# A hybrid flow trunk on one core: tile order of small products, row blocks of modulation weights, resident tables and the place of gate loads

## The chip, the cores and the metric

The kernel runs on one core of a Trainium2 chip. The metric is the device time of one execution in microseconds (us), the median of three runs. The core has five engines with an instruction queue each: PE (matrix products, with weight loads shown as PEld), DVE (vector), ACT (scalar and activation), POOL (general vector work) and SP, which here only issues transfers. The program sets the order of each queue. Sixteen DMA engines move data between memory (HBM) and the on-chip memory (SBUF). PE's results go to PSUM, in banks.

## What is computed

One step of a two-layer trunk over 128 context tokens and 1024 latent tokens, 1024 wide. Each layer: RMSNorm, shift and scale from the conditioning (`mod`), one combined input projection, three parallel branches, each with its own SiLU gate, and an output projection with RMSNorm, gate and residual.

```python
mod = silu(cond) @ w_mod + b_mod                    # shift, scale, gate
h = rmsnorm(x, g_pre) * (1 + scale) + shift
z = h @ w_in
o_a = windowed_attention(rope(q), rope(k), v, sink) * silu(ag)   # A
o_b = u * (w_s @ layernorm(v) + b_s) * silu(bg)                  # B
# C, gated DeltaNet in chunks of 64 tokens, forward and backward:
t_mat = inverse(eye + strict_lower(beta * k @ k.T * decay))
u, w = t_mat @ (v * beta), t_mat @ (k * beta * exp(gc))
for each chunk:                                                  # the scan
    v_new = u - w @ state
    o = q_dec @ state + a_qk @ v_new
    state = state * exp(g_last) + k_dec.T @ v_new
x = x + gate * rmsnorm(concat(o_a, o_b, o_c) @ w_out, g_post)
```

Outputs are the context and latent tokens, the context keys and values of each layer and the final states.

## The kernel before

Tokens are nine tiles of 128 (`NT`, eight latent and one context tile, `CTX`). Large products use a pair of 16-bit parts for each factor, so three matmuls per block of the contraction; `load_w` brings weights through one of two staging buffers (`st`, 4 KB per partition, L155) and ACT (L160) and DVE (L161) split them. The small products of branch C are in 32 bits; each of them is two instructions on PE, with two weight loads. `X` holds the normalized input of all tiles and is read by every projection (`proj_tok`, L165, matmuls at L170).

A layer has two strands of work. `chain` is branch C: `c_gates` and `c_features`, then `scan`. In `scan`, each of two head groups needs the inverse of its chunk matrices: `diagonals` (L479) turns 32 x 32 diagonal blocks, `solve` (L503) inverts them in 31 dependent DVE steps, and `inverses` (L516) makes the off-diagonal blocks by two products of 32 x 32 blocks. In these, `sides` (L522) lists four combinations of direction and half; each uses other 32 rows and 32 columns of PE's array, and for each side all L blocks j (16 for the latent chunks of a head group, 4 for the context) follow each other (L525 to L528 and L541 to L544). Between the products ACT and POOL write the negated diagonal inverses into W (L537, L539). Then `steps` (L549) runs through the chunks, 18 per head group.

`fill` is everything else that PE can do meanwhile: `b_branch`, `c_gate`, and `attention` with, in layer 0, the modulation of layer 1 (`mod`, L210) threaded through it. `b_gate` (L823) is done twice, for 128 columns each: it loads its weights into `wb` and projects the nine tiles. `both` orders them: the heavy work (attention) runs until `light` has an entry, then a `b_gate` comes. `lat_solve` (L661) adds the entry in the tenth step of the first head group's solve (`LT`) and in the third step of the second's. `merge` (L1124) interleaves chain and fill by the costs that they yield. From the program so written a scheduler with a time model makes the order in which each engine gets its instructions, so an edit in one place can shift work elsewhere.

`mod` loads w_mod as 256 rows by 512 columns (k2 = 0 to 3), two row blocks per load; row block k uses column tile k % 4 of the array (L245 to L249). In the prologue, for the first two parts of layer 0, 16 loads have buffers of their own (`wm`); the 32 others go through `st`.

The rotary table is loaded per token tile, 64 KB at a time, into `rt`: nine times for the keys (L1018) and 18 times for the queries (L909) of each layer, from SP's queue. The transposes of the attention's probabilities (`PT<-P`, L953) are issued there too. CK, 640 columns of triangle masks and a block of ones, is loaded once in the prologue (`masks`, L123) and stays; its last reader in a layer is L405. `out_layer` (L1044) multiplies by w_out, reading the branches' results back from memory into `OTm` (L1054), two buffers. The pools on the "right" side form a stack; `c0` lies at its bottom and holds the first head group's q and k (`cqk[0]`).

## Time and profile before

| | us |
|---|---|
| median of three runs | 1471.59 |
| lowest, highest | 1468.35, 1475.64 |
| the profiled execution | 1462.98 |
| its span in the trace | 1460.2 |
| PE, DVE, ACT, POOL busy | 1307.0, 941.5, 616.9, 613.4 |

The profile is one execution. Its page gives busy times, forty slices of the span, the queues, the chain of work that ended last, and the costliest groups. Longer answers come from the trace: groups by source line, waits, stretches. A name like `ps<-sv,NA` says which tile an instruction writes and which it reads. Layer 0 is at about 75 to 774 us, layer 1 from there to the end; the last part of each layer is `out_layer`. Small products of the inverses stand at about 295, 360, 535 (layer 0) and 994, 1050, 1224 us (layer 1).

### The profile page before, as it was taken

Reading aid. Unit: us, or ns where it says so; the run is one execution under the profiler, and the core shown is the slowest. Engines: PE = TensorE matmul, PEld = TensorE weight load, DVE = VectorE, ACT = ScalarE, POOL = GpSimd, SP = SyncE. Lnnn points to the kernel's source line nnn. Section 1 sums busy time; section 2 is a strip of 40 time slices with the busy share of each in tenths; the row PEclk is TensorE's granted clock in tenths of the full one; section 3 lists DMA queues with packets and bytes.
Section 4 is the critical chain, followed back from the end, with each engine's and each line's share of the span. In section 5 each row is a group of like instructions: output and inputs, shape, how many; then the busy total and the mean of one; then the engine's idle time right before and its main releaser. Section 6 shows DMA issues by size and latency. Waiting matters only on the chain.

```text
span 1460.2 us, 38255 instructions
## 1 busy us (share of the span) xinstructions
PE 1307.0 (90%) x15479; PEld 1009.7 (69%) x15479; DVE 941.5 (64%) x2230; ACT 616.9 (42%) x1411; POOL 613.4 (42%) x818
## 2 busy tenths in 40 slices
PE   6899989899998699959897999999898769987997
PEld 2665567666667587748786655678787658865886
DVE  2865689987646666753446587687875485767333
ACT  2733454434646116732333444332566313665211
POOL 0761245435556135742132432631668403666200
PEclk8999999999999898969998999999999988998999
DMA  9331044839865117673332122242276311877552
GB/s 358 120 80 55 24 113 106 180 105 222 162 171 87 39 32 144 120 221 76 120 131 84 32 63 68 73 95 64 55 142 120 60 49 40 157 115 166 130 181 103
DMA packets 301562, 162.92 MB, mean 112 GB/s; under 512 B 212622, under 2 KB 277938, under 8 KB 301386
## 3 DMA queue, kind: packets, MB, share of 16 engines
q1 hardware_dynamic: 264301, 127.94, 37.4%
q10 hardware_dynamic: 37085, 32.55, 7.6%
q8 instruction: 121, 1.98, 0.6%
q14 instruction: 55, 0.45, 0.1%
HBM read 95.78 MB, written 24.28 MB: 82 GB/s over the span
## 4 chain that ended last, share of the span: by engine, by line
PE 54%; DVE 14%; DMA 13%; issue 7%; POOL 6%; ACT 4%; SPq 1%; ACTq 0%; DVEq 0%; POOLq 0%
PE ps L170 16%; PE ps L1072 12%; PE ps L312 6%; DMA PT<-P 4%; DMA st<-in_w_in_dram 2%; DMA st<-in_w_mod_dram 2%; PE ps L967 2%; POOL P L951 2%; PE ps L249 2%; DVE y L319 1%; DVE sv L512 1%; PE ps L543 1%; PE ps L527 1%; DVE sv L510 1%; DVE wg L161 1%
## 5 line engine op out<-in xcount | busy, mean ns | idle before, releaser
L170 PEld LDWEIGHTS <-X 128*128 128x128 f16 x3888 | 349.6, 100 | 101.2 <-issue 39.3
L170 PE MATMUL ps<-wg,X 128*128 128x256 f16 x2592 | 328.6, 280 | 10.5 <-DVE wg L161 3.9
L951 POOL TENSOR_TENSOR P<-sS,P 128x512 f16<-128x512 f32 (+2 forms) x144 | 150.9, 1053 | 100.9 <-ACT sS L949 100.2
L1072 PEld LDWEIGHTS <-OTm 128*128 128x128 f16 x1728 | 169.1, 99 | 30.5 <-DMA OTm<-mix_d 8.8
L1072 PE MATMUL ps<-wo,OTm 128*128 128x256 f16 x1296 | 152.1, 276 | 7.6 <-DMA OTm<-mix_d 7.6
L312 PE MATMUL ps<-X,wg 128*128 128x512 f16 (+1 forms) x864 | 146.1, 329 | 1.8 <-ACT wg L160 1.4
L946 DVE CUSTOM_DVE_ANT_0 sS<-ps,am,nsk 128x512 f32<-128x512 f32 (+2 forms) x144 | 95.1, 669 | 49.1 <-POOL P L951 24.6
L948 ACT ACTIVATE P<-sS,nmx 128x512 f16<-128x512 f32 (+2 forms) x144 | 94.0, 660 | 73.0 <-DVE nmx L946 67.4
L312 PEld LDWEIGHTS <-wg 128*128 128x128 f16 x864 | 74.0, 99 | 69.1 <-ACT wg L160 1.8
L170 PE MATMUL ps<-wb,X 128*128 128x256 f16 x864 | 102.5, 279 | 14.4 <-ACT wb L160 12.5
L949 ACT ACTIVATE sS<-sS,nmx 128x512 f32<-128x512 f32 (+2 forms) x144 | 95.1, 660 | 4.2 <-DVE OTA L1001 0.4
L145 POOL TENSOR_TENSOR rs<-ms,mhalf 128x1 f32<-128x1 f32 x36 | 20.7, 576 | 171.9 <-DVE ms L1081 103.7
L967 PE MATMUL ps<-Vt,PT 128*128 128x128 f16 (+1 forms) x992 | 67.9, 211 | 22.8 <-DMA PT<-P 21.8
L319 DVE SCALAR_TENSOR_TENSOR y<-zT,cw,y 128x1156 f32<-128x1156 f32 x48 | 68.9, 1439 | 27.4 <-ACT y L317 26.8
L512 DVE TENSOR_TENSOR sv<-sv 128x31 f32<-128x31 f32 (+15 forms) x186 | 78.4, 421 | 4.1
L967 PEld LDWEIGHTS <-PT 128*128 128x128 f16 x992 | 51.1, 100 | 41.6 <-DMA PT<-P 29.7
L510 DVE TENSOR_TENSOR sv<-sv 128x31 f32<-128x31 f32 (+15 forms) x186 | 74.8, 402 | 4.0
L942 PE MATMUL ps<-KT,qT 128*128 128x128 f16 (+2 forms) x272 | 68.6, 269 | 0.0
L288 DVE TENSOR_SCALAR hf<-ps,AB 128x128 f32<-128x128 f32 x117 | 39.7, 402 | 39.3 <-PE ps L281 39.0
L1075 ACT ACTIVATE sq<-ps 128x512 f32<-128x512 f32 x36 | 21.3, 594 | 99.8 <-PE ps L1072 56.8
L941 PE MATMUL ps<-KT,qT 128*128 128x128 f16 (+2 forms) x272 | 60.3, 271 | 3.6 <-DVE nmx L946 1.8
L161 DVE SCALAR_TENSOR_TENSOR wg<-st,wg 128x1024 f16<-128x1024 f32 x44 | 56.0, 1280 | 10.6 <-ACT wg L160 10.4
(265 smaller groups left out, 2723.8 us busy)
## 6 DMA issues: line engine op xcount, KB each, us to landing
st<-in_w_in_dram ACTq DMA_DIRECT2D x38, 512.0 KB
st<-in_w_mod_dram SPq DMA_DIRECT2D x32, 512.0 KB
OTm<-mix_d SPq DMA_DIRECT2D x18, 512.0 KB
wm<-in_w_mod_dram SPq DMA_DIRECT2D x16, 512.0 KB
xt<-in_x_sample_dram SPq DMA_DIRECT2D x16, 512.0 KB
st<-in_w_out_dram ACTq DMA_DIRECT2D x16, 512.0 KB
mix_d<-OTA SPq DMA_DIRECT2D x36, 128.0 KB
xs<-xt SPq DMA_DIRECT2D x9, 512.0 KB
```

The source lines that it names most:

```text
L161: V.scalar_tensor_tensor(dst[:, 4 * h:4 * h + 4, 1, :cols], s, WS, hi, op0=ALU.mult, op1=ALU.subtract)
L170: T.matmul(ps, X[:, t, k, a, :], wg[:, k, b, c0:c0 + n], start=(i == 0), stop=(i == 23))
L312: T.matmul(ps[:, 0:n], wg[:, k, b, 128 * hg:128 * hg + 128], X[:, t0:t1, k, a, :], start=(i == 0), stop=(i == 23))
L319: V.scalar_tensor_tensor(y, zT[:, tap:tap + 1156], cw[:, tap * 6 + ct:tap * 6 + ct + 1], y, op0=ALU.mult, op1=ALU.add)
L510: V.tensor_tensor(t3, m3[:, 0:m, m:m + 1].to_broadcast([128, m, w]), y3[:, m:m + 1, m:32].to_broadcast([128, m, w]), op=ALU.mult)
L512: V.tensor_tensor(y3[:, 0:m, m:32], y3[:, 0:m, m:32], t3, op=ALU.subtract)
L946: V.tensor_tensor_reduce(sS[:, 0:nk], ps[:, 0:nk], mk, -0.125, nsk[:, hh:hh + 1], ALU.add, ALU.min, accum_out=nmx[:, h:h + 1])
L948: S_.activation(P16[:, 0:nk], sS[:, 0:nk], AF.Exp, bias=nmx[:, h:h + 1], scale=-1.0)
L949: S_.activation(sS[:, 0:nk], sS[:, 0:nk], AF.Exp, bias=nmx[:, h:h + 1], scale=-1.0, accum_out=sm[:, h:h + 1])
L951: G.tensor_tensor(P16[:, nk:2 * nk], sS[:, 0:nk], P16[:, 0:nk], op=ALU.subtract)
L967: T.matmul(pops[:, 128 * h:128 * h + n], PT[:, a * nb + j, :], Vt[:, blist[j], kv].rearrange("p s d -> p (s d)")[:, 0:n], start=(i == 0), ...
L1072: T.matmul(ps[:, 256 * i:256 * i + 256], OTm[:, k, a, :], w[:, k, b, :], start=(n == 0), stop=(n == 23))
```

## The change

In `inverses` the two loops are exchanged: for each block j the four sides follow each other, so that consecutive matmuls use four different tiles of the array. In `mod`, loads through `st` take 512 rows by 256 columns, four row blocks, and each feeds four matmuls of 256 columns on the four column tiles; the `wm` loads are as before. CK leaves the permanent pool and is loaded by `c_gates` in each layer, ahead of `sab`; the prologue loads only the part that makes `triL16`, beside the other masks. The rotary table of all nine tiles is loaded once per layer when `attention` starts (`rts`, 4608 bytes per partition). `b_gate` yields after its weight load is written down; `both` then lets heavy work of a cost of 8.0 (first gate) or 1.0 (second) go ahead of the rest of it. The second gate's entry in `light` comes before the solve's first step instead of in its third. The output of `b_gate` goes out in one transfer per pair of tiles. `OTm` becomes the halves of one tile `OT2` that takes the place of `cqk[0]`, and `c0` stays open through `out_layer`.

```diff
@@ -40,6 +40,7 @@
 PRO = 1
 LT = 9
 AHEAD = 6
+EARLY = (8.0, 1.0)
 FILL = 0.9
 
 
@@ -110,10 +111,6 @@
     V.tensor_copy(id16, ident)
     idb = per.tile([128, 128], BF16, name="idb")
     V.tensor_copy(idb, ident)
-    CK = per.tile([128, 640], F32, name="CK")
-    triI = [CK[:, 0:128], CK[:, 128:256]]
-    triL = [CK[:, 256:384], CK[:, 384:512]]
-    bdones = CK[:, 512:640]
     selc = per.tile([128, 2], F32, name="selc")
     V.reduce_sum(selc, ident.rearrange("p (j c) -> p c j", c=32)[:, 0:2, :], axis=AX.X)
     triIc16 = per.tile([128, 2, 64], F16, name="triIc16")
@@ -121,12 +118,12 @@
     triL16 = per.tile([128, 2, 128], F16, name="triL16")
 
     def masks():
-        dma(CK, cst[:, 0:640])
-        ctmp = stg.tile([128, 256], F32, tag="st", name="ctmp")
-        dma(ctmp, cst[:, 640:896])
+        ctmp = stg.tile([128, 512], F32, tag="st", name="ctmp")
+        dma(ctmp[:, 0:256], cst[:, 640:896])
+        dma(ctmp[:, 256:512], cst[:, 256:512])
         G.tensor_copy(triIc16, ctmp[:, 0:128].rearrange("p (r c) -> p r c", r=2))
         G.tensor_copy(mneg, ctmp[:, 128:256].rearrange("p (r c) -> p r c", r=2))
-        G.tensor_copy(triL16, CK[:, 256:512].rearrange("p (r c) -> p r c", r=2))
+        G.tensor_copy(triL16, ctmp[:, 256:512].rearrange("p (r c) -> p r c", r=2))
 
     mhalf = per.tile([128, 18], F32, name="mhalf")
     G.memset(mhalf, -0.5)
@@ -239,14 +236,20 @@
                 for k2 in range(4):
                     if wmp is not None and part < 2:
                         st = wmp.tile([128, 4, 256], F32, tag="wm", name=nm("wm"), bufs=16)
-                    else:
-                        st = stg.tile([128, 4, 256], F32, tag="st", name=nm("st"))
-                    s = st.rearrange("p a b -> p (a b)").rearrange("p (k c) -> p k c", k=2)
-                    dma(s, w_mod[l, 256 * k2:256 * k2 + 256, 512 * cb:512 * cb + 512].rearrange("(k p) c -> p k c", p=128))
-                    for kk in range(2):
-                        k = 2 * k2 + kk
-                        j = k % 4
-                        T.matmul(ps[32 * j:32 * j + 32, :], csp[:, k, :], s[:, kk, :], start=(k < 4), stop=(k >= 4))
+                        s = st.rearrange("p a b -> p (a b)").rearrange("p (k c) -> p k c", k=2)
+                        dma(s, w_mod[l, 256 * k2:256 * k2 + 256, 512 * cb:512 * cb + 512].rearrange("(k p) c -> p k c", p=128))
+                        for kk in range(2):
+                            k = 2 * k2 + kk
+                            j = k % 4
+                            T.matmul(ps[32 * j:32 * j + 32, :], csp[:, k, :], s[:, kk, :], start=(k < 4), stop=(k >= 4))
+                        continue
+                    ch, kq = k2 // 2, k2 % 2
+                    c0 = 512 * cb + 256 * ch
+                    st = stg.tile([128, 4, 256], F32, tag="st", name=nm("st"))
+                    dma(st, w_mod[l, 512 * kq:512 * kq + 512, c0:c0 + 256].rearrange("(k p) c -> p k c", p=128))
+                    for j in range(4):
+                        T.matmul(ps[32 * j:32 * j + 32, 256 * ch:256 * ch + 256], csp[:, 4 * kq + j, :], st[:, j, :],
+                                 start=(kq == 0), stop=(kq == 1))
                 mp = mp_.tile([128, 512], F32, tag="mp", name=nm("mp"), bufs=2 if PIPE else 1)
                 (V.tensor_copy if wmp is not None and part < 2 else S_.copy)(mp, ps)
                 todo.append((part, cb, mp))
@@ -354,6 +357,11 @@
 
     def c_gates(l, cp, gp, out):
         GB = cp.tile([128, 2, 2, 9, 4], F32, name=nm("GB"))
+        CK = gp.tile([128, 640], F32, name="CK")
+        dma(CK, cst[:, 0:640])
+        triI = [CK[:, 0:128], CK[:, 128:256]]
+        triL = [CK[:, 256:384], CK[:, 384:512]]
+        bdones = CK[:, 512:640]
         wab = gp.tile([128, 8, 2, 16], F16, name="wab")
         sab = gp.tile([128, 8, 16], F32, name="sab")
         dma(sab, w_in[l, :, C_AB:C_AB + 16].rearrange("(k p) c -> p k c", p=128))
@@ -522,8 +530,8 @@
             sides = [(r, half, 64 * half + (0 if half == r else 32), 64 * half + (32 if half == r else 0))
                      for r in range(2) for half in range(2)]
             ps = psw()
-            for (r, half, p1, p2) in sides:
-                for j in range(L):
+            for j in range(L):
+                for (r, half, p1, p2) in sides:
                     T.matmul(ps[p2:p2 + 32, 32 * j:32 * j + 32], W[p1:p1 + 32, r, j, p2 % 64:p2 % 64 + 32],
                              PQ[1 if half == r else 0][p1:p1 + 32, L * r + j, :], start=True, stop=True)
             C_ = ep[:, 3328:3840]
@@ -538,8 +546,8 @@
                     else:
                         G.tensor_scalar(dst, src, -1.0, None, op0=ALU.mult)
             ps = psw()
-            for (r, half, p1, p2) in sides:
-                for j in range(L):
+            for j in range(L):
+                for (r, half, p1, p2) in sides:
                     T.matmul(ps[p1:p1 + 32, 32 * j:32 * j + 32], C_[p2:p2 + 32, 32 * j:32 * j + 32],
                              W[p2:p2 + 32, r, j, p2 % 64:p2 % 64 + 32], start=True, stop=True)
             for (r, half, p1, p2) in sides:
@@ -660,9 +668,11 @@
 
         def lat_solve(hg, sv):
             M, Y = diagonals(sv, Ws[hg], 16)
+            if hg:
+                light.append(hg)
             yield 4.0
             for i, cost in enumerate(solve(sv, M, Y)):
-                if i == (2 if hg else LT):
+                if not hg and i == LT:
                     light.append(hg)
                 yield cost * share[5 if hg else 2]
             inverses(sv, Ws[hg], 16, Y)
@@ -825,6 +835,7 @@
         cs = slice(128 * k, 128 * k + 128)
         w = bp.tile([128, 8, 2, 256], F16, name=nm("wb"), bufs=1)
         load_w((w_in[l, :, C_BU + 128 * k:C_BU + 128 * k + 128], w_in[l, :, C_BG + 128 * k:C_BG + 128 * k + 128]), 256, w)
+        yield 0.0
         sc = IWS * IWS * IWS * 0.5
 
         def out(ts, th):
@@ -836,8 +847,7 @@
             src = pt[:, 0:128 * n].rearrange("p (q c) -> p q c", c=128)
             S_.activation(ot[:, 0:n, 0, :], src, AF.Copy, scale=sc)
             V.scalar_tensor_tensor(ot[:, 0:n, 1, :], src, sc, ot[:, 0:n, 0, :], op0=ALU.mult, op1=ALU.subtract)
-            for j, t in enumerate(ts):
-                dma(mix_d[t, :, 4 + k].rearrange("p s c -> p (s c)"), ot[:, j].rearrange("p s c -> p (s c)"))
+            dma(mix_d[ts[0]:ts[0] + n, :, 4 + k].rearrange("t p s c -> p t (s c)"), ot[:, 0:n].rearrange("p t s c -> p t (s c)"))
 
         prev = None
         for ts in pairs:
@@ -883,6 +893,8 @@
             am = p1.tile([128, 640], F32, name="am")
             dma(am, amask)
             sk = p1.tile([128, 8], F32, name="sk")
+            rts = p1.tile([128, 9, 128], F32, name="rts")
+            dma(rts, rope.rearrange("t p c -> p t c"))
             ordert = [CTX] + list(range(8))
             dma(sk, attn_sink[l].partition_broadcast(128))
             nsk = p1.tile([128, 8], F32, name="nsk")
@@ -905,8 +917,7 @@
                 pq = psp()
                 proj_tok(pq[:, 0:256], t, wq)
                 proj_tok(pq[:, 256:512], t, wa)
-                rt = p2.tile([128, 128], F32, tag="rt", name=nm("rt"))
-                dma(rt, rope[t])
+                rt = rts[:, t, :]
                 qa = rope_tile(p2, pq[:, 0:256], 4, rt)
                 th = p2.tile([128, 256], F32, tag="ga", name=nm("ga"), bufs=5)
                 S_.activation(th, pq[:, 256:512], AF.Tanh, scale=IWS * 0.5)
@@ -1014,8 +1025,7 @@
                         for t in ordert:
                             ps = psp()
                             proj_tok(ps[:, 0:256], t, wkv)
-                            rt = p2.tile([128, 128], F32, tag="rt", name=nm("rt"))
-                            dma(rt, rope[t])
+                            rt = rts[:, t, :]
                             ka = rope_tile(p2, ps[:, 0:128], 2, rt)
                             vf = p2.tile([128, 256], F32, tag="ga", name=nm("vf"), bufs=5)[:, 0:128]
                             S_.activation(vf, ps[:, 128:256], AF.Copy, scale=IWS)
@@ -1041,16 +1051,17 @@
                         weigh(*pend.pop(0))
                     finish(p2, *prev.pop())
 
-    def out_layer(l, wo, nextAB):
+    def out_layer(l, wo, c0, nextAB):
         last = l == NL - 1
         with pool(f"o1{l}", 1, "right") as p1, pool(f"o2{l}", 2, "right") as p2:
             wo.append(load_w(w_out[l, :, 512:768], 256, p1.tile([128, 8, 2, 256], F16, name=nm("wo"))))
             wo.append(load_w(w_out[l, :, 768:1024], 256))
             GG, todo = {}, []
+            OT2 = c0.tile([128, 2, 8, 2, 128], F16, tag="cq0", name=nm("OT2"))
 
             for ti, t in enumerate((3, 4, 2, 5, 1, 6, 0, 7, 8)):
                 cond = 1 if t == CTX else 0
-                OTm = p1.tile([128, 8, 2, 128], F16, tag="OTm", name=nm("OTm"), bufs=2)
+                OTm = OT2[:, ti % 2]
                 dma(OTm, mix_d[t])
                 if cond not in GG:
                     g = p1.tile([128, DM], F32, tag="GG", name=nm("GG"), bufs=2)
@@ -1156,7 +1167,7 @@
         rs = ExitStack()
         ctx.enter_context(rs)
         c0 = rs.enter_context(pool(f"c0{l}", 1, "right"))
-        cqk = [q.tile([128, 9, 2, 128], F32, name=nm("cqk")) for q in (c0, cp)]
+        cqk = [q.tile([128, 9, 2, 128], F32, tag=f"cq{i}", name=nm("cqk")) for i, q in enumerate((c0, cp))]
         cv_ = [q.tile([128, 9, 128], F32, name=nm("cv")) for q in (c0, cp)]
         nxt = [None, None]
         light = []
@@ -1194,7 +1205,16 @@
                     yield got
                 elif k < 2:
                     with pool(f"bg{l}{k}", 2, "right") as bp:
-                        yield from b_gate(l, bp, k)
+                        gate = b_gate(l, bp, k)
+                        yield next(gate)
+                        n = 0.0
+                        while n < EARLY[k]:
+                            got = next(heavy, None)
+                            if got is None:
+                                break
+                            n += got
+                            yield got
+                        yield from gate
                     k += 1
                 else:
                     break
@@ -1204,8 +1224,8 @@
             for _ in pairs:
                 next(fl)
         merge(chain(), fl)
+        out_layer(l, wo, c0, nxt[1])
         rs.close()
-        out_layer(l, wo, nxt[1])
         keep.close()
         ls.close()
         vt, AB = nxt
```

## Rows read from the trace of the kernel before

**Rows 1.** The page: busy times and instructions; busy tenths in forty slices.
```profile
PE 1307.0 (90%) x15479; PEld 1009.7 (69%) x15479; DVE 941.5 (64%) x2230; ACT 616.9 (42%) x1411; POOL 613.4 (42%) x818
...
PE   6899989899998699959897999999898769987997
```

**Rows 2.** Stretches: length, busy PE, PEld, DVE, ACT, POOL; clock, DMA share, GB/s.
```profile
236.00:360.00 124.00, 114.14 (x1093) 77.99 (x1091) 113.89 (x289) 52.42 (x132) 52.47 (x64) 0.99 0.68 159
360.00:377.00 17.00, 17.00 (x348) 13.85 (x346) 6.24 (x16) 7.95 (x20) 7.59 (x8) 1.00 0.67 133
494.00:535.00 41.00, 31.67 (x293) 27.66 (x294) 36.99 (x88) 7.77 (x16) 5.61 (x6) 0.83 0.18 53
535.00:555.00 20.00, 20.00 (x317) 16.40 (x314) 7.55 (x15) 8.13 (x16) 9.57 (x16) 0.74 0.21 53
613.00:653.00 40.00, 23.84 (x398) 19.35 (x398) 22.94 (x57) 16.39 (x36) 20.28 (x32) 0.73 0.73 198
1049.00:1068.00 19.00, 18.51 (x336) 16.50 (x337) 9.15 (x24) 9.92 (x22) 9.30 (x9) 0.82 0.32 50
1171.00:1187.00 16.00, 4.81 (x83) 4.04 (x84) 12.04 (x29) 4.80 (x7) 0.76 (x2) 0.70 0.08 22
1224.00:1244.00 20.00, 20.00 (x326) 16.80 (x323) 7.68 (x22) 8.01 (x22) 5.97 (x14) 0.74 0.30 72
```

**Rows 3.** Groups by line: xcount | busy us, mean ns | idle before, releasers.
```profile
L543 PE MATMUL ps<-NA,sv 32*32 32x32 f32 x512 | 18.0, 200 | 0.0
...
L527 PE MATMUL ps<-sv,NA 32*32 32x32 f32 x512 | 17.4, 199 | 1.3 <-DVE sv L520 1.3
...
L527 PE MATMUL ps<-sv,NAc 32*32 32x32 f32 x64 | 1.8, 194 | 0.0
...
L249 PEld LDWEIGHTS ps<-st,csp 128*32 128x32 f32 x128 | 4.3, 109 | 14.3 <-DMA st<-in_w_mod_dram 10.8 <-issue 2.6
```

**Rows 4.** Timeline, weight loads and POOL: start us, us, engine, line, operation.
```profile
308.09 0.16 PEld L249 LDWEIGHTS ps<-st,csp 128*32 128x32 f32 x8 [0.21 <-issue]
...
357.24 4.60 POOL L539 TENSOR_SCALAR NA<-sv 32x512 f32<-32x512 f32 x3
...
360.17 3.82 PEld L527 LDWEIGHTS ps<-sv,NA 32*32 32x32 f32 x128 [0.21 <-issue]
...
379.52 0.31 PEld L566 LDWEIGHTS ps<-ident,qk 64*64 64x64 f32 x8 [0.21 <-issue]
```

**Rows 5.** Timeline of PE: two groups of modulation matmuls.
```profile
308.09 1.07 PE L249 MATMUL ps<-st,csp 128*32 128x512 f32 x8
...
370.01 1.05 PE L249 MATMUL ps<-st,csp 128*32 128x512 f32 x4
```

**Rows 6.** The chain that ended last, two weight loads: start us, us, what.
```profile
190.44 4.86 DMA st<-in_w_in_dram
...
316.86 3.86 DMA st<-in_w_mod_dram
```

**Rows 7.** Waits of SP (us, times, longest), then two pieces of the chain.
```profile
SPq L909 <- DVE ru L870: 25.5, 10, 5.5
...
943.84 3.65 DMA sk<-in_attn_sink_dram
...
1149.65 2.54 DMA rt<-in_rope_dram
```

**Rows 8.** Waits of PE, the chain, PE's timeline at the second gate.
```profile
PE ps L170 <- ACT wb L160: 12.5, 3, 5.7
...
1182.68 1.98 DMA out_dram<-S
...
1186.03 0.80 PE L170 MATMUL ps<-wb,X 128*128 128x256 f16 x3 [5.74 <-ACT wb L160]
```

**Rows 9.** The chain at the start of out_layer and of layer 1.
```profile
650.02 3.55 DMA OTm<-mix_d
...
771.15 2.28 DMA sab<-in_w_in_dram
```

## The prediction

> **What bounds the kernel now.** I read the page first: PE is busy for 1307.0 of 1460.2 us, DVE for 941.5, and the forty slices show PE at 9 nearly everywhere, with dips [rows 1]. So a microsecond of PE work taken away should be worth most of a microsecond, except where something else is late. The table of stretches shows where [rows 2]. From 236 to 360 us DVE is busy 113.9 of 124 us beside PE's 114.1: the 31-step solve and the attention's vector work share the limit. At 360 to 377 and 535 to 555, around the small products of the inverses, PE is busy the whole time, and what waits for them (the scan's steps) can't go on. At 494 to 535 and 1171 to 1187 PE has holes; at 613 to 653 the scan's own chain of latencies ends the layer with PE busy 23.8 of 40 us, so work saved ahead of it is partly lost there. The waits and the chain that ended last name the holes: the gate weights, the modulation loads, a rotary table.
>
> **Small products in another order.** The two products of `inverses` cost 17.4 + 18.0 us for the four 16-block calls and 1.8 us each for the two 4-block calls (one of these two equal rows is shown): 39.0 us of PE for 1152 matmuls, each with its weight load (every source matmul is two instructions) [rows 3]. Today all blocks of one tile of the array follow each other: 128 loads in 3.82 us, 30 ns each [rows 4]. The change lets four tiles with different rows and columns alternate. Nearest rows: eight loads on two alternating 64x64 tiles take 0.31 us with the last one's tail, about 24 ns each without it although each load is twice as wide [rows 4]; eight on four column tiles of the modulation take 0.16 us, and with a last load of 0.109 us off that is 0.05 us for seven, 7 ns [rows 3, 4]. And eight modulation matmuls on four tiles last 1.07 us where four on two tiles last 1.05 [rows 5]: tiles run beside each other. The bounds are 30 ns (no gain) and 7 ns (1152 x 7 = 8.1 us, 31 us saved). No row shows how fast PE's sequencer supplies 128 pairs in a row, so I take 12 ns, nearer to the four-tile row since that is the same case: 13.8 us, 25 us of PE saved. A loss of 1 us is not excluded, since the first four matmuls now need the inputs of all four sides. Not all of it reaches the end. The second product needs POOL's copies at L539, which in one instance end at 357.24 + 4.60 = 361.84, only 1.7 us after the first product began [rows 4], and attention matmuls stand between the two in PE's queue. I count 60%: **15 us** (-1 to 31).
>
> **Clock around them.** The granted clock is 0.74 at 535 to 555 and 1224 to 1244, and 0.82 at 1049 to 1068 [rows 2]; with levels of 1.2 and 2.4 GHz, 0.74 of 20 us means 10.4 us at the low one. In these stretches PE had just run these 32x32 products; at 360 to 377 the same products ran and the clock stayed at 1.00. Shorter products might keep it up: at most half of (10.4 + 10.4 + 6.8) us = 14 us; I take **4** (0 to 14).
>
> The Trainium skill, TensorEngine Tiling (Array Packing), section Restrictions and Gotchas, says that different row tiles cannot use the same PSUM bank at the same time, and all four tiles here write one bank. By that rule the products would stay at 30 ns and the sum would lose these 19 us. The trace speaks against it as far as it goes: the two 64-row tiles of L566 also write one bank, at 24 ns for doubly wide loads [rows 4]. The same skill, TensorE: Matmul & The Clock Gate, section "Wait — 56ns, not 53.3ns?", gives a floor of about 25 ns from start to start of matmuls however small; by it a product would take 128 x 25 = 3.2 us, an estimate from that page, and the saving would be a sixth. The eight loads at 7 ns contradict it for short bursts; no row shows a long one.
>
> **Modulation in four row blocks.** 32 loads change (the `st` ones; the 16 of the prologue's `wm` don't). A load now feeds four instructions on two tiles that hold PE for 1.05 us [rows 5]. Half the columns on four tiles makes it about 0.6 (0.15 to 0.2 of a group is the tail of its last instruction, the rest halves), by the x8 row, in which four tiles cost no more than two. The timeline has 26 such groups and 3 of eight, where two loads came together and nothing is gained: 26 x 0.45 = 11.7 us of PE. Nine groups lie after 360 us, where PE is the limit (4 us); 17 lie in 236 to 360, where DVE limits as well; of their 7.6 us I count a fifth. The load's runs shrink from 2 KB to 1 KB. A 512 KB w_mod load of 2 KB runs took 3.86 us on the chain and a w_in load of 1 KB runs 4.86 [rows 6]; both had other traffic beside them, so I count 0.5 us lost in all. **5 us** (-6 to 11.7; the low end is 32 loads that land 0.2 us later each with PE waiting).
>
> **Rotary tables.** 54 loads (27 per layer) leave SP's queue. One of them stands on the chain with 2.54 us [rows 7], and before such loads SP waited 25.5 us for the buffer's last reader (L870) [rows 7], with transposes of P and qT queued behind; most of that was hidden. I take 3 (0 to 8). Against it: 576 KB per layer now stand ahead of `sk` in SP's queue, and `sk` is already late once, 3.65 us on the chain, with DVE's `nsk` and all DVE work behind it waiting [rows 7]. A load of about that size takes 4 to 5 us by itself; overlapped with `sk` I take 2 (0 to 8 for two layers). Net **+1**. The gate's output goes out in one DMA per pair, 36 issues become 20: off the chain, nothing.
>
> **Early gate weights.** PE waited 12.5 us for the first half of `wb` [rows 8], 5.74 of it before 1186.03 in layer 1 and nearly as much before 504.4 in layer 0. The loads had been issued long before; what held the conversion back was the tile's memory: on the chain the store of the final state, `out_dram<-S`, 1.98 us, ends right before it in layer 1 [rows 8]. That stays. What is new is that one unit of attention (a head or a projection, 1 to 5 us of PE) comes between the load and the gate's matmuls, and fills the hole. For the first gate, 8 units come between, for a wait of some 1 us. So 4 of 5.7 twice, plus 1, two thirds of it at the end: **6 us** (0 to 13). The attention moved ahead carries DVE work beside the solve; at 494 to 535 DVE has 4 us free [rows 2], which covers it; without that cover it costs 2 us per layer.
>
> **Constants.** CK is now loaded in each layer ahead of `sab` in SP's queue. In layer 1 `sab` is on the chain with 2.28 us [rows 9]; 320 KB ahead of it cost at most the 3.86 us of a 512 KB load [rows 6] and at least one issue, about 0.4. The `wab` matmuls wait for X anyway, so I take 1 per layer: **-2** (0 to -8). `triI` and the others are needed much later.
>
> **OT2.** The two halves of one tile replace two buffers. If halves are followed separately, as for X, this costs nothing: what hides a load is the previous tile's matmuls.
>
> **Sum.** 15 + 4 + 5 + 1 + 6 - 2 = 29 us. The profiled execution took 1462.98 us (span 1460.2), so it would take 1434; the median of the three runs is 1471.59, 8.6 above it, and 29 below that is **1443**.
>
> **Rivals.** (1) *The array or its supply does not take four tiles at once.* For: one bank, and no long row. Against: rows 4 and 5. The products stay as they are: 1443 + 19 = 1462. (2) *PE is freed where it only waits.* For: 613 to 653, where the chain and not PE is late, and DVE's 92% at 236 to 360. Then a quarter of the sum stays, 7 us: 1465. Against: PE fully busy around all products. (3) *Everything counts*: products near 7 ns, the clock up, gate holes closed: 31 + 8 + 8 + 3 + 10 - 2 = 58 us at most; with part of it, 1420. (4) *Slower: OT2 is followed as one tile.* Then from the second tile of `out_layer` on, each load waits until the matmuls of the tile before have read the other half. A load takes 3.55 us on the chain [rows 9]; 8 per layer exposed, 16 x 3.55 = 57 us, less the 29: 1500. It decides if the load of one tile is issued after the last matmul of the tile before. Against: slices of X are written in the prologue while matmuls read others, so slices are followed one by one there.
>
> **How the numbers follow.** The kernel's runs tell 0.5% (7 us) from no change. Forecast (1430 to 1457): 0.46. (3): 0.12. (1): 0.14, two thirds of it beyond 0.5%. (2): 0.12, within or just beyond it. (4): 0.08. The remaining 0.08 is for instruction orders of the planner, which I can't price, all slower. Faster 0.46 + 0.12 + 0.09 + 0.02 = 0.69, same 0.15, slower 0.16. The range from 1420 to 1476 leaves out (4), the unpriced cases and a little of (3).
>
> **What would show it.** Each product's 128 loads should take about 1.5 us instead of 3.82, with starts on four tiles; 3.2 or more means rival 1. Clock near 1 at the four stretches. Modulation groups about 0.55 us. PE's wait for `wb` under 4 us in all. No wait on `rt`. `sk` and `sab` no more than 2 us later. OTm loads issued during the tile before. The forecast is wrong if PE's busy time falls by over 25 us and the span doesn't, or if the second product still starts some 6 us after the first.

## The result and the profile after

The changed kernel takes **1431.39 us** (median of four runs, 1427.35 to 1437.79) against 1473.62 for the kernel before (four runs beside it): a ratio of **0.969, 95% interval 0.966 to 0.973**. The forecast was 1443, between 1420 and 1476, and 29 us gained; the medians give 42. The two profiled executions differ by 28.6 us of span (1460.2 and 1431.6), since the profiled execution of before was among the shortest of that kernel's; the comparisons below go by medians and ratios.

The page after: span, busy times, PE's forty slices and the granted clock in tenths.

```profile
span 1431.6 us, 38343 instructions
...
PE 1267.3 (89%) x15607; PEld 979.3 (68%) x15607; DVE 940.3 (66%) x2230; ACT 613.7 (43%) x1411; POOL 604.3 (42%) x818
...
PE   6899979778989789969898999999899768987997
...
PEclk8999999989999989989999999999999989999999
```

PE's busy time fell by 39.7 us [rows 1], more than the span. PE's time that isn't busy (span less busy) went from 153.2 to 164.3 us. The groups of PE by line after: xcount | busy us, mean ns | idle before.

```profile
L251 PE MATMUL ps<-st,csp 128*32 128x256 f32 x256 | 23.6, 414 | 13.5 <-DMA st<-in_w_mod_dram 13.5
...
L551 PE MATMUL ps<-NA,sv 32*32 32x32 f32 x512 | 6.9, 194 | 0.0
L535 PE MATMUL ps<-sv,NA 32*32 32x32 f32 x512 | 6.2, 204 | 4.1 <-DVE sv L528 4.1
...
L535 PE MATMUL ps<-sv,NAc 32*32 32x32 f32 x64 | 0.9, 194 | 0.0
```

L535 and L551 are the old L527 and L543: 39.0 us became 14.9 (the second 4-block row is equal to the one shown). L251 is the old L249 with half the columns: 23.6 us where it was 31.4 in the same view of before:

```profile
L249 PE MATMUL ps<-st,csp 128*32 128x512 f32 x128 | 31.4, 619 | 8.8 <-DMA st<-in_w_mod_dram 8.8
```

The stretches around the large products and the two second gates: length, busy PE, PEld, DVE, ACT, POOL, clock, DMA share, GB/s.

```profile
343.00:373.00 30.00, 26.57 (x482) 17.37 (x480) 17.37 (x42) 18.68 (x43) 16.43 (x15) 0.94 0.84 177
494.00:528.00 34.00, 24.34 (x227) 21.16 (x228) 30.45 (x73) 5.64 (x10) 2.22 (x3) 0.80 0.20 59
530.00:550.00 20.00, 20.00 (x409) 16.85 (x408) 14.52 (x31) 10.82 (x21) 12.82 (x17) 1.00 0.23 59
1020.00:1040.00 20.00, 15.91 (x375) 12.89 (x373) 17.23 (x37) 13.14 (x31) 13.25 (x13) 0.91 0.50 74
1150.00:1165.00 15.00, 5.85 (x45) 4.38 (x46) 13.10 (x31) 2.65 (x4) 0.00 (x0) 0.54 0.22 60
1196.00:1216.00 20.00, 15.04 (x363) 12.24 (x362) 11.57 (x34) 11.68 (x29) 7.36 (x16) 0.91 0.48 107
```

The clock around the second head group's products is 1.00 and 0.91 where it was 0.74 twice [rows 2]. The two holes before the second gate are still there, at 0.80 and 0.54.

Waits of PE after (line, what it waited for: us in all, times, longest), and the chain that ended last just before the second gate of layer 1 (start, us, what):

```profile
PE ps L978 <- DMA PT<-P: 31.7, 33, 2.5
PE ps L251 <- DMA st<-in_w_mod_dram: 13.5, 8, 7.5
PE ps L167 <- ACT wb L157: 11.3, 2, 5.6
...
PE ps L1083 <- DMA OT<-mix_d: 3.6, 3, 1.7
```

```profile
1157.01 1.98 DMA out_dram<-S
1159.15 1.06 ACT wb L157
1160.24 1.24 DVE wb L158
1161.52 3.55 PE ps L167 x17
```

The wait for `wb` went from 12.5 to 11.3 us only [rows 8]: the store of the final state still ends right before ACT's conversion. The wait for w_mod rose from 8.8 to 13.5, the one for the transposed probabilities (`PT`) from 21.8 to 31.7.

**A way to split the time.** Each run has its span and its mean granted clock. Span times clock is the time with the low-clock stretches counted at half; span times (1 - clock) is the rest, called the *loss* here. It is a way of counting, not a law. Over 47 runs of the kernel before, the span falls by some 11 us for each 0.01 of clock (correlation -0.72); if all of the loss were time lost it would fall by some 16 (1473 / 0.943 x 0.01). So the name claims too much: part of the loss falls where PE waits anyway. In the trace of the changed kernel, cut into slices of 10 us, PE's busy time in each times (1 - its clock) makes 44 us, of 67 us of loss. Medians of the runs, in us; the last column is the ratio to the kernel before in the same comparison, and its interval:

| kernel | time | span x clock | loss | ratio |
|---|---|---|---|---|
| before (14, 16 and 17 runs in the three comparisons) | 1473 to 1478 | 1387 to 1388 | 85 to 87 | 1 |
| changed | 1431.4 | 1363.5 | 67 | 0.969 (0.966 to 0.973) |
| side_major | 1473.0 | 1376 | 94 | 0.998 (0.995 to 1.001) |
| old_mod | 1452.1 | 1370 | 80 | 0.984 (0.978 to 0.989) |
| gate_old | 1444.8 | 1372 | 71 | 0.980 (0.976 to 0.984) |
| first_gate_late | 1446.2 | 1373 | 71 | 0.981 (0.977 to 0.984) |
| rt_tiles | 1433.7 | 1370 | 62 | 0.972 (0.968 to 0.976) |
| state_copy | 1436.3 | 1364 | 72 | 0.974 (0.970 to 0.977) |
| out_per_tile | 1432.0 | 1359 | 72 | 0.972 (0.967 to 0.976) |
| two_tiles | 1434.5 | 1366 | 66 | 0.973 (0.968 to 0.978) |
| three_times | 1487.3 | 1390 | 95 | 1.008 (1.005 to 1.010) |
| dense_before | 1458.8 | 1376 | 78 | 0.988 (0.984 to 0.993) |
| before_products | 1455.0 | 1382 | 74 | 0.988 (0.982 to 0.993) |
| before_mod | 1469.4 | 1383 | 86 | 0.997 (0.994 to 0.999) |

Effects below are differences of ratios times 1474 us; against the changed kernel they are known to some 7 to 9 us either way, both intervals put together. Nearly half of the whole gain, 18 to 20 of 42 to 45 us, is loss that went (85 to 87, now 67).

### The profile page after: what moved, and what is told of

It is laid out like the page before. It is cut to its first block, busy times and chain, and to the rows that moved or that the text cites. A ratio compares the mean times of both kernels' runs of the same rounds, so it can differ in the third digit from the quotient of the medians.

```text
span 1431.6 us, 38343 instructions
## 1 busy us (share of the span) xinstructions
PE 1267.3 (89%) x15607; PEld 979.3 (68%) x15607; DVE 940.3 (66%) x2230; ACT 613.7 (43%) x1411; POOL 604.3 (42%) x818
## 4 chain that ended last, share of the span: by engine, by line
PE 46%; DVE 19%; DMA 14%; POOL 8%; issue 8%; ACT 4%; SPq 1%; DVEq 0%; POOLq 0%; ACTq 0%
PE ps L167 12%; PE ps L1083 12%; PE ps L315 7%; DMA PT<-P 6%; POOL P L962 3%; DVE sv L518 3%; DVE sv L520 3%; DMA st<-in_w_in_dram 3%; PE ps L728 2%; PE ps L978 1%; DVE sS L957 1%; DVE y L322 1%; PE ps L601 1%; DVE wg L158 1%; PE ps L590 1%
## 5 line engine op out<-in xcount | busy, mean ns | idle before, releaser
L1083 PEld LDWEIGHTS <-OT 128*128 128x128 f16 x1728 | 169.5, 99 | 26.5 <-DMA OT<-mix_d 4.1
L1083 PE MATMUL ps<-wo,OT 128*128 128x256 f16 x1296 | 153.7, 278 | 3.6 <-DMA OT<-mix_d 3.6
L167 PE MATMUL ps<-wb,X 128*128 128x256 f16 x864 | 101.2, 278 | 12.2 <-ACT wb L157 11.3
L978 PE MATMUL ps<-Vt,PT 128*128 128x128 f16 (+1 forms) x992 | 66.5, 208 | 32.8 <-DMA PT<-P 31.7
L518 DVE TENSOR_TENSOR sv<-sv 128x31 f32<-128x31 f32 (+15 forms) x186 | 74.5, 401 | 4.2
L520 DVE TENSOR_TENSOR sv<-sv 128x31 f32<-128x31 f32 (+15 forms) x186 | 72.7, 391 | 4.5
L157 ACT ACTIVATE wg<-st 128x1024 f16<-128x1024 f32 x44 | 45.3, 1054 | 40.5 <-DMA st<-in_w_in_dram 30.6
L1086 ACT ACTIVATE sq<-ps 128x512 f32<-128x512 f32 x36 | 21.3, 593 | 95.1 <-PE ps L1083 54.7
```

Of the source, the lines that this page charges most:

```text
L167: T.matmul(ps, X[:, t, k, a, :], wg[:, k, b, c0:c0 + n], start=(i == 0), stop=(i == 23))
L518: V.tensor_tensor(t3, m3[:, 0:m, m:m + 1].to_broadcast([128, m, w]), y3[:, m:m + 1, m:32].to_broadcast([128, m, w]), op=ALU.mult)
L520: V.tensor_tensor(y3[:, 0:m, m:32], y3[:, 0:m, m:32], t3, op=ALU.subtract)
L978: T.matmul(pops[:, 128 * h:128 * h + n], PT[:, a * nb + j, :], Vt[:, blist[j], kv].rearrange("p s d -> p (s d)")[:, 0:n], start=(i == 0), ...
L1083: T.matmul(ps[:, 256 * i:256 * i + 256], OTm[:, k, a, :], w[:, k, b, :], start=(n == 0), stop=(n == 23))
```

## The products: undone, and alone

**side_major.** The two loops back in the old nesting, in the changed kernel:

```diff
-            for j in range(L):
-                for (r, half, p1, p2) in sides:
+            for (r, half, p1, p2) in sides:
+                for j in range(L):
```

> The changed kernel with the two loops of the inverses back in the old nesting (all blocks of one side after each other), everything else as changed. Theory T1 (the products' own time is the main gain; 24 us of PE are saved and 60% or more of them reach the end, and the clock around them rises): PE is busy 22 to 26 us longer, a run of 128 loads takes 3.8 us again instead of 1.1, the time is 1431 + 15 to 24 = 1446 to 1455 us, and the low-clock stretches at about 540 and 1230 us come back. Rival R1 (PE was freed where it only waits, and the gain came from the order of work that the other parts bring): PE busy longer by as much, but the time 1431 to 1437.

Measured: 1473.0 us, 42 more than the changed kernel. The whole gain is gone, twice as much as T1 expected. PE is busy 1305.9 us, 38.6 more, of which the products are 26.7 (14.9 in the changed kernel, 41.6 here with two rows of 1.8 for the small calls):

```profile
L551 PE MATMUL ps<-NA,sv 32*32 32x32 f32 x512 | 19.5, 202 | 0.0
L535 PE MATMUL ps<-sv,NA 32*32 32x32 f32 x512 | 18.5, 203 | 4.5 <-DVE sv L528 4.5
```

The other 12 us are the same work taking longer, which fits the lower clock (0.939 for 0.953). Of the 42 us, 13 are span times clock and 27 are loss. The stretches around its four large products, and then one call's weight loads in the timelines of this kernel and of the changed one:

```profile
345.00:375.00 30.00, 30.00 (x402) 21.58 (x399) 13.02 (x27) 12.85 (x28) 12.80 (x11) 0.77 0.52 129
540.00:560.00 20.00, 20.00 (x323) 16.31 (x322) 8.22 (x18) 7.49 (x14) 10.66 (x15) 0.75 0.15 35
1050.00:1070.00 20.00, 18.32 (x299) 15.82 (x300) 8.98 (x19) 9.01 (x20) 9.78 (x9) 0.63 0.12 22
1232.00:1252.00 20.00, 20.00 (x353) 17.34 (x352) 6.51 (x19) 6.96 (x17) 6.08 (x14) 0.91 0.24 49
```

```profile
542.10 3.82 PEld L535 LDWEIGHTS ps<-sv,NA 32*32 32x32 f32 x128 [0.21 <-DVE th L864]
```

```profile
535.91 1.18 PEld L535 LDWEIGHTS ps<-sv,NA 32*32 32x32 f32 x128 [0.21 <-DVE th L864]
```

The first two lie between the same neighbours (`th` at L864 ends the wait before both). In the old order the loads start 29 ns apart, in the new one 8.4 ns (1.07 us from the first to the last of 128). In these four stretches the old order loses 30 x 0.23 + 20 x (0.25 + 0.37 + 0.09) = 21 us to the clock, the changed kernel 30 x 0.06 + 20 x (0 + 0.09 + 0.09) = 5 us: these 16 us are most of the 22 or 23 by which the two profiled executions differ in loss (0.061 x 1472.4 = 90 and 0.047 x 1431.6 = 67).

**before_products.** The same exchange in the kernel before, and nothing else.

```diff
-            for (r, half, p1, p2) in sides:
-                for j in range(L):
+            for j in range(L):
+                for (r, half, p1, p2) in sides:
```

> The kernel before with the loops of the inverses exchanged and nothing else. T1: PE busy falls by 24 us and the time by 15 to 24 us: 1450 to 1459 (ratio 0.984 to 0.990). Rival R1 (the gain needs the other parts): less than 6 us, 1468 or more.

Measured: 1455.0, 18 us faster than before (11 to 26), as T1 said; PE is busy 19.7 us less. R1 falls here and in side_major: the products carry gain in either kernel. But they carry 18 us in one and 42 in the other: the parts don't add up.

## What the slow products did to the clock

The old order holds PE longer and leaves most of the array idle. Which of the two brings the clock down? Two kernels hold PE for longer in the new order.

**three_times.** Each product three times over:

```diff
-            for j in range(L):
+            for j in [j for _ in range(3) for j in range(L)]:
```

> The changed kernel with each of the inverses' products done three times over in the new order (the same blocks into the same places), so that a 16-block call holds PE for about 3 x 1.1 = 3.3 us, nearly as long as the 3.8 us of the old order; everything else as changed. With the old order in the changed kernel the time was 1473, the span times the granted clock 1376 us (changed: 1364) and the rest, lost to the low clock, 94 us (changed: 67). Theory T2 (what the old order costs beside PE's time is the clock: 32x32 products one tile at a time bring it down): span times clock 1373 to 1376, the loss stays at 65 to 72, the time 1440 to 1447. Rival R4 (a longer product brings the loss however its tiles are ordered, by later work and other gaps): the loss rises to 85 to 94 and the time to 1460 or more. Rival R5 (PE's time here is hidden): 1434 or less.

Measured: 1487.3, a loss of 94.5. By the numbers this is R4, but the run didn't make what it was meant to. PE's weight loads of one call, in the timeline:

```profile
1057.18 2.04 PEld L535 LDWEIGHTS ps<-sv,NA 32*32 32x32 f32 x233 [2.44 <-DVE sv L528]
1061.73 1.23 PEld L535 LDWEIGHTS ps<-sv,NA 32*32 32x32 f32 x128 [2.51 <-issue]
1065.74 0.41 PEld L535 LDWEIGHTS ps<-sv,NA 32*32 32x32 f32 x23 [2.79 <-issue]
```

After 233 loads no new one starts for 2.51 us, and after 128 more for 2.79, with nothing in the profile that it waits for; such waits are 12.6 us at L535 and 14.4 at L551. A call took 8 to 11 us instead of 3.3, with holes in it, so it says nothing on a full queue of small products. What PE waits for there no run shows.

**dense_before.** Full-array work instead:

```diff
             ps = psw()
+            for _ in range(3 if L == 16 else 1):
+                w = 448 if L == 16 else 128
+                T.matmul(ps[:, 0:w], ident, C_[:, 0:w], start=True, stop=True)
```

(and the same with `PQ[0]` ahead of the first product).

> The changed kernel with dense work ahead of each of the inverses' products: three full 128x128 by 448-column matmuls in 32 bits (one of 128 columns for the small calls) into the places that the product then overwrites, so that PE is held about as long as the old order held it (some 2.7 us more per large call, an estimate from the modulation's 512-column instructions), but with a full array; the products stay in the new order. Theory T2 (what costs the clock is PE holding on to small products, one tile or stalled, with most of the array idle; as much dense work doesn't): PE busy 20 to 25 us longer, span times clock 1378 to 1390, the loss stays at 60 to 72, the time 1443 to 1458. Rival R4 (any longer hold there raises the loss, by what comes later and by other gaps): the loss at 85 or more, as in the old order (94) and the threefold products (94.5), and the time at 1465 or more.

Measured: 1458.8 us, 28 more than the changed kernel, 14 less than the old order; the intervals don't overlap. The dense work held PE for 21.3 us (the 2.7 us per large call that I had estimated were 2.5). Span times clock is 1376, as in the old order, so PE's time costs 12 to 13 us in both, some 60% of the dense work's and half of the products', give or take the 5 us that another order of work is worth (last section of runs). The loss is 78, between the two theories. The stretches around its products:

```profile
345.00:375.00 30.00, 28.82 (x490) 18.65 (x488) 19.95 (x45) 19.52 (x44) 18.34 (x19) 0.96 0.95 192
535.00:555.00 20.00, 19.84 (x383) 15.34 (x382) 10.74 (x26) 10.16 (x18) 11.91 (x17) 1.00 0.32 87
1030.00:1050.00 20.00, 16.70 (x375) 11.93 (x377) 16.19 (x34) 13.57 (x31) 12.53 (x13) 1.00 0.47 73
1210.00:1230.00 20.00, 18.14 (x365) 13.14 (x363) 8.90 (x31) 10.59 (x29) 8.41 (x17) 1.00 0.36 65
```

Here the clock is 0.96 and three times 1.00: with 21.3 us of PE time put in, 1 us is lost, against 21 in the old order with 26.7. So T2 holds where it speaks, for these two executions: around the products the clock falls with the small products one tile at a time and not with the time PE is held. The 11 us of loss that the dense kernel has over the changed one lie elsewhere in the execution, and for them R4 may be right; where they come from stays open.

Nor does every stretch follow T2. In the kernel before, the clock stayed at 1.00 at 360 to 377 with the old order [rows 2], so its four stretches lose some 14 us and not 21. With the new order and nothing else, in before_products, they lose 7:

```profile
345.00:375.00 30.00, 25.59 (x421) 15.75 (x420) 19.27 (x49) 16.56 (x37) 14.90 (x14) 0.90 0.82 173
535.00:555.00 20.00, 20.00 (x420) 16.80 (x418) 14.21 (x29) 12.37 (x23) 14.12 (x18) 1.00 0.44 93
1045.00:1065.00 20.00, 17.26 (x387) 13.70 (x387) 14.73 (x31) 11.24 (x26) 13.01 (x12) 0.91 0.53 82
1220.00:1240.00 20.00, 16.17 (x372) 13.19 (x370) 11.40 (x33) 11.90 (x30) 8.18 (x17) 0.89 0.54 117
```

The first stretch is 0.90 here and 1.00 before; in the other three the new order goes with the higher clock (1.00, 0.91 and 0.89 for 0.74, 0.82 and 0.74). So the order of the tiles is not all that decides; what else must come to it no run shows.

## How many tiles it takes

**two_tiles.** Sides 0 and 3 in turn, then sides 1 and 2:

```diff
-            for j in range(L):
-                for (r, half, p1, p2) in sides:
+            for q in (sides[0:1] + sides[3:4], sides[1:3]):
+              for j in range(L):
+                for (r, half, p1, p2) in q:
```

> The changed kernel with the products on two tiles in turn instead of four (sides 0 and 3, then sides 1 and 2; in each pair other rows and other columns). T1 (a tile takes a pair each 30 ns, and tiles run beside each other, until the supply of instructions ends it at about 8.5 ns): a pair each 15 ns, 128 loads in 1.9 to 2.1 us, PE busy 7 to 9 us longer, time 1434 to 1439. Rival R2 (what matters is only that the next product isn't on the same tile): 128 loads in 1.1 us, time as changed, 1431. Rival R3 (PSUM's one bank or a floor of 25 ns a matmul comes in when a tile's turn comes sooner): 3.2 us or more, 1440 or more.

```profile
534.22 2.01 PEld L536 LDWEIGHTS ps<-sv,NA 32*32 32x32 f32 x128 [0.21 <-DVE th L866]
```

Measured: the same call's 128 loads in 2.01 us, so 15 ns apart: 29, 15 and 8.4 ns with one, two and four tiles, each tile taking one every 29 to 34 ns. T1 holds; R2 (1.1 us) and R3 (3.2 us) fall. The products hold PE 7.8 us longer. The time, 1434.5, is 5 us above the changed kernel by the ratios, within the intervals, and the loss is the same (66): already two tiles keep the clock.

These paces are those of a clock of 1.00. One call of the changed kernel comes after PE has waited 4.07 us, at a granted clock of 0.50, and takes 14 ns a pair:

```profile
1024.97 1.83 PEld L535 LDWEIGHTS ps<-sv,NA 32*32 32x32 f32 x128 [4.32 <-issue]
```

## The modulation

**old_mod.** The loads of 256 rows by 512 columns back, in the changed kernel.

```diff
-                    dma(st, w_mod[l, 512 * kq:512 * kq + 512, c0:c0 + 256].rearrange("(k p) c -> p k c", p=128))
-                    for j in range(4):
+                    dma(s, w_mod[l, 256 * k2:256 * k2 + 256, 512 * cb:512 * cb + 512].rearrange("(k p) c -> p k c", p=128))
+                    for kk in range(2):
```

> The changed kernel with the modulation's loads as before (256 rows by 512 columns, two column tiles), everything else as changed. T1 (modulation is worth about 5 us): PE busy 8 us longer in the modulation's groups, time 1434 to 1438. Rival R1 (the saved PE time came back as waits for w_mod loads of 1 KB runs: these waits grew by 5 us in the trace of the changed kernel): time 1428 to 1433, with the wait for w_mod near 9 us instead of 13.5.

Measured: 1452.1, 21 us slower (6 in span times clock, 13 in loss), four times what T1 expected. The wait for w_mod falls to 5.0 us, further than R1 said, and that doesn't help. The groups' busy time is 31.4 again, 7.8 more, but PE's busy time as a whole is 20.4 more: the rest is other work, which fits the lower clock (0.940 for 0.953).

**before_mod.** The new loads in the kernel before, and nothing else.

```diff
-                    for kk in range(2):
...
+                    for j in range(4):
```

> The kernel before with the modulation's loads in four row blocks and nothing else. Taken out of the changed kernel this part cost 21 us (two thirds of it clock loss), while all parts but the products together gave 3 us. Theory T5 (parts work on the clock together: with the slow products in place the modulation's gain is lost again): 0 to 8 us faster than before, PE busy 6 to 9 us less. Rival R11 (the parts add up): 15 us faster or more, 1463 or less.

Measured: ratio 0.9965, 5 us faster (1 to 9), with no change in the loss (86). T5 holds in the time and R11 falls; PE's busy time fell by 3.5 us only, not 6 to 9: the groups gained 7.4, and the first products, still in the old order, took 4.6 more. So this part is worth 5 us alone and 21 with all the other parts in place; which of them makes the difference wasn't tried. side_major shows the same from the other end: all parts but the products save 11 us of span times clock and lose 7 of them again to the clock. Why the clock gives back what the other parts save, while the old products are in, no run here shows.

## The gate's weights

**gate_old.** Both gates' loads where they were.

```diff
-                        gate = b_gate(l, bp, k)
-                        yield next(gate)
...
-                        yield from gate
+                        yield from b_gate(l, bp, k)
```

> The changed kernel with the gates' weights loaded where the gate's matmuls follow (no unit of other work in between) and the second gate's entry in the third step of the solve, as before; everything else as changed. Theory T3 (the early load didn't fill the hole: PE still waits 5.63 us twice for wb in the changed kernel, because the tile's memory is held by the store of the final state; only a wait of 1 us is gone): time within 5 us of the changed one, 1427 to 1436. Rival R6 (the step as predicted, 6 us): 1437 to 1442, with PE's wait for wb near 12.5 us in three places.

**first_gate_late.** All else as changed.

```diff
-EARLY = (8.0, 1.0)
+EARLY = (0.0, 1.0)
```

> The changed kernel with no other work between the first gate's weight load and its matmuls (8.0 becomes 0.0 in EARLY); the second gate as changed. In the changed kernel PE waits 7.49 us before 293.7 for a w_mod load, because the first gate's early loads hold both staging buffers meanwhile. Theory T4 (that wait is a price of the early load and counts): the wait for w_mod falls from 13.5 to about 6 us in all and the time by 3 to 8 us, to 1423 to 1428. Rival R10 (PE's idle time only moves: it was 151 to 155 us of gaps over 0.1 us in every kernel so far but the threefold one): the same time within 4 us, or up to 13 us slower as the kernel with both gates late (1445).

Measured: 1444.8 and 1446.2, 15 and 16 us slower. So the second gate's new place, on which the prediction put nearly all of this part, is worth nothing that can be told (tried only with the first gate late), and the first gate's, on which it put 1 us, is worth 15. T3's time fails in gate_old (R6's wait of 12.4 us in three places is there, its time isn't), and T4 fails: in first_gate_late the wait for w_mod did fall to 5.6 us, and the kernel is slower, a little beyond R10's upper end. Most of it is span times clock (1373 for 1363.5). The second gate of layer 1 in the timelines of the late and of the changed kernel:

```profile
1173.79 0.80 PE L167 MATMUL ps<-wb,X 128*128 128x256 f16 x3 [5.63 <-ACT wb L157]
```

```profile
1160.26 0.80 PE L167 MATMUL ps<-wb,X 128*128 128x256 f16 x3 [5.63 <-ACT wb L157]
```

At that point the late kernel is 13.5 us behind. At the second gate of layer 0 it wasn't behind at all (505.4 and 505.5), at `out_layer`'s first matmul of layer 0 3.6 us (642.7 and 639.1), at the first gate of layer 1 4.2 (978.5 and 974.3): most of the delay comes with the first scan of layer 1. By the end 8.1 us of it are left in these two executions (1439.7 and 1431.6), half of what the medians show, with PE's time that isn't busy 172.4 us instead of 164.3 at the same 1267.3 us of work. No single wait has it. The reading that fits is that attention done ahead of the gate is attention that needn't be done beside and after the scan's steps, where it goes slowly; it is argued, not shown.

**state_copy.** POOL copies the final state into a tile of its own, which is then stored:

```diff
+            Sf = SF[hg]
+            G.tensor_copy(Sf, Sc)
             for d in range(2):
-                dma(new_s[0, l, 1 - d, h0:h0 + 2].rearrange("h d v -> d h v"), Sc[64 * d:64 * d + 64])
+                dma(new_s[0, l, 1 - d, h0:h0 + 2].rearrange("h d v -> d h v"), Sf[64 * d:64 * d + 64])
```

> The changed kernel with the final state of each head group copied by POOL into a small tile of its own, which is what is stored; so the pool of the scan's tiles is free as soon as that copy is done and no DMA holds the memory that wb takes over. Theory T3: the wait for wb shrinks by the store's issue and its 1.98 us, from 5.63 to 2 to 3.7 us in both places, ACT's conversion of wb no longer stands behind the store, and the time falls by 3 to 6 us: 1425 to 1429. Rival R7 (something else ends as late, such as the weight transfer or ACT's queue): the wait stays above 5 us and the time at 1431.

```profile
504.96 0.80 PE L167 MATMUL ps<-wb,X 128*128 128x256 f16 x3 [3.12 <-ACT wb L157]
```

Measured: the wait falls from 5.63 to 3.12 us in both places, 6.2 in all, which shows that the store of the state held the tile's memory for that long; what the other 3.12 us wait for was not tried. But the time is 1436.3, by its interval no better than the changed kernel, with span times clock the same (1364). PE's time that isn't busy is 162.4 us, hardly less than 164.3: five microseconds of a hole closed came back as other waits.

## The rest, and a control

**rt_tiles.** The rotary table tile by tile, for queries and keys.

```diff
-                rt = rts[:, t, :]
+                rt = p2.tile([128, 128], F32, tag="rt", name=nm("rt"))
+                dma(rt, rope[t])
```

> The changed kernel with the rotary table loaded tile by tile again (54 loads), the resident table left out; everything else as changed. By the prediction's terms (3 us gained less 2 us for the late sk): 1432 to 1435, with SP waiting some 25 us in all for rt's buffer. Rival R8 (waits on rt only ever took the place of others): 1428 to 1431. Rival R9 (other orders of work change the clock's loss by more than the term): the span times the clock stays at 1362 to 1367 while the loss moves by over 6 us.

**out_per_tile.** The gate's output stored tile by tile.

```diff
-            dma(mix_d[ts[0]:ts[0] + n, :, 4 + k].rearrange("t p s c -> p t (s c)"), ot[:, 0:n].rearrange("p t s c -> p t (s c)"))
+            for j, t in enumerate(ts):
+                dma(mix_d[t, :, 4 + k].rearrange("p s c -> p (s c)"), ot[:, j].rearrange("p s c -> p (s c)"))
```

> The changed kernel with the gate's output stored tile by tile as before (36 transfers instead of 20), everything else as changed. No theory gives this edit a cost on the path; it shows what another order of the same work, as the program's scheduler makes it after a small edit, is worth by itself: 1427 to 1436 if that is little, and a loss that moves by more than 6 us or a span times clock that moves by more than 5 us if the other runs' small differences are of that kind.

Measured: 1433.7 and 1432.0; both ratios' intervals overlap the changed kernel's, and nothing of 3 us can be told from nothing. So rt_tiles lands where the prediction's terms put it, with SP waiting 22.2 us again for the query's buffer, but doesn't decide between them and R8; R9 fails as stated, since span times clock moved out of its range. Span times clock went up by 6 and the loss down by 5 in the first, and down by 5 and up by 4 in the second: another order of the same work moves each of the two by about 5 us, against each other. Differences of that size in the table mean nothing; those of the products, the modulation, the first gate and the dense work are larger in time and outside the intervals. With only two such controls an effect of order can't be ruled out for them.

The resident table has the price that was forecast: its transfer now stands on the chain at the start of layer 1's attention, where the late `sk` stood with 3.65 us [rows 7] (chain of the changed kernel):

```profile
923.70 5.96 DMA rts<-in_rope_dram
```

## Why the prediction was right, and where it was not

**Products.** PE saved 24.1 us (forecast 25), at 8.4 ns a pair instead of the assumed 12 within an unbroken call at full clock; other work between the pieces of a call, each piece with a tail of its last instruction, and one call at half the clock make up the difference. The forecast's sign of being wrong, a second product that still starts some 6 us after the first, came in one call of four (7.9 us, 348.3 to 356.2); in the others it starts 4.2 to 4.7 us after, where it was 8.5 to 9.2 in the kernel before. The 60% of it that was counted (15 us) was too much: by span times clock 13 us count in the changed kernel, and 5 in the kernel before, each give or take some 5. The nearest row for the pace was the four-tile one, and it held for 128 in a row. By the bank rule of the Trainium skill, TensorEngine Tiling (Array Packing), section Restrictions and Gotchas, there would have been no gain; four tiles write one bank here at 8.4 ns a pair, so the measurement decides against it for these products.

**Clock around them.** This is the term that was mis-sized: 4 us (0 to 14), and the loss fell by 13 us in before_products and rose by 27 in side_major. The direction and the place were right (0.74 to 1.00 and 0.91 around the second head group's products), but I capped it at half of the low-clock time in three stretches of one execution, one whose clock was among the highest of the kernel's runs.

**Modulation.** 5 us forecast, 5 measured alone, 21 in the changed kernel. The groups fell by 7.8 us where 11.7 were counted: a group of eight takes 0.64 us at full clock, not 0.6, and a group that other work breaks up pays its tail twice (two matmuls of one last 0.62 us, the other six 0.63). The loads' price was there, 13.5 for 8.8 us of waiting, 7.49 of it once. old_mod and first_gate_late take that price away and are slower all the same, so taking it away is worth less than what goes with it.

**Rotary tables, constants, OT2.** Net +1; 3 measured for the tables, with an uncertainty of 8, so nothing. The chain shows `sab` with 3.06 us for 2.28 in layer 1, under 1 us as counted. The rival in which OT2 is followed as one tile did not come: PE's wait for it fell from 7.6 to 3.6 us. CK and OT2 were not tried by themselves.

**Early gate weights.** 6 us forecast, 15 measured, by another way, so this term was right in sign by luck: "comes between the load and the gate's matmuls, and fills the hole" failed. The hole of 5.63 us stayed in both layers (11.3 us of waiting for `wb`, where under 4 were to show the step), and the gain came with the first gate, for which 1 us was counted.

**The sum** came out near the measurement (29 of 42) with parts that are not those measured: side_major, old_mod and gate_old, each by itself, take away 42 + 21 + 15 = 78 us of a gain of 42 to 45. That the sum was near is in part luck. What the forecast lacked is that the parts meet in one quantity, the granted clock: in span times clock the three take away 13 + 6 + 9 = 28 us where 24 were gained, which is nearly a sum; in loss they take away 27 + 13 + 4 = 44 us where 18 to 20 were gained. Why the parts don't add up there stays open. Of the rivals, (1) and (4) fell; (2) fell, since undoing the products costs all of the gain; (3) had most of the mechanisms, the clock above all, though not the closed holes, and its 1420 is as far below the median as the forecast is above it.

## What to carry to other kernels

Small matmuls on single tiles of the array should alternate over tiles with other rows and other columns: a pair each 29, 15 or 8.4 ns with one, two or four. Where PE bounds the kernel, weigh an edit by the granted clock as well as by time: a stretch in which PE is busy with little of its array can cost more in the clock than in its own length (27 us of loss beside 13 here), and the price of one part then depends on which others are there. Closing a hole in front of PE was worth nothing here (state_copy), since PE's idle time as a whole hardly fell.

## What the runs showed of the hardware

Four 32x32 tiles take weight loads and matmuls beside each other into one PSUM bank, at 8.4 ns a pair over 128 pairs at a clock of 1.00, and 14 ns at 0.50; each tile takes one in 29 to 34 ns at 1.00. A long run of such pairs breaks: in three_times PE stood for up to 3.0 us at a time, 27 us in all, for nothing that the profile shows; in seven of the eight large calls it stood first after 211 to 264 pairs, in most of them again 128 pairs later. Not only longer runs break: in before_products one call of 128 stood for 2.7 us before its last five pairs. And the mean granted clock of one kernel differs between its runs, 0.93 to 0.95 over 47 runs of before, with spans of 1461 to 1484 us along with it, so that one profiled execution is a poor base for a sum of a few per cent.
